# A hybrid encoder block on one core: spread norm factors read in PSUM, and the second FFN's first three weight pieces loaded and split in common tiles during the recurrence

## The chip, the cores and the metric

One core of a Trainium2 chip runs the whole block. The metric is the device time of one execution in microseconds (us); the kernel before takes 1086.48 us, the median of three runs (1085.79 to 1087.56).

## The reference

One residual layer on 512 tokens of width 1024, all in float32: a half-step SwiGLU FFN, a token mixer of two head groups (a gated delta rule and a latent attention), and a second half-step SwiGLU FFN. Each of the three starts with an RMS norm of x that is scaled and shifted per column.

```
h = _rms(x) * (1.0 + s1) + sh1
x = x + 0.5 * g1 * ((silu(h @ gate) * (h @ up)) @ ffn1_w_out)
h = _rms(x) * (1.0 + s2) + sh2
x = x + g2 * (concat(gated_delta_rule(h), latent_attention(h)) @ w_out)
h = _rms(x) * (1.0 + s3) + sh3
x = x + 0.5 * g3 * ((silu(h @ gate) * (h @ up)) @ ffn2_w_out)
```

The FFN is 2816 wide. The delta rule carries a state over the sequence and is worked out in blocks of 128 tokens.

## The kernel before, in words

The activations lie transposed, 128 features on the partitions and 512 tokens along the free axis: x is eight tiles `xT[0..7]`. A product in float32 is done as three matmuls of rounded halves (`mm3`, lines 258 to 261): each operand is split in a high part (a cast on ScalarE, called ACT in the profile) and a low part (operand minus high part on VectorE, DVE). Weights come in **pieces** of 1024 rows by 128 columns: one DMA fills a raw tile `wr`, then line 191 (ACT) casts it to `wh` and line 192 (DVE) subtracts to `wl`. These three tags have four buffers each, in a pool of their own, used in turn. All other 128 by 512 tiles come out of one common pool of 56 ("slots"), used in turn too. PSUM has three accumulators (`psa`) and five auxiliary tiles (`psb`).

The list of pieces is written down in `plan_units`; `prefetch(n)` emits load and split of the next ones until n are ready, and `next_unit` hands one out.

The **norm** before the mixer and before the second FFN is done in two halves of 256 tokens, so that it overlaps the matmuls around it (`norm_half`, line 472). A half goes: column sums of the squares by matmul (line 506), 1/rms on GpSimd (line 177), a diagonal matrix of it (`dg`, line 426, DVE), a matmul of ones by `dg` that spreads the factors over all partitions (line 434, into PSUM), a copy of the result to the slot tile `rb` (line 436, ACT). Then `modulate` does for each of the eight `kt`: x times scale times `rb` (`hm`, line 452, DVE), the shifted sum rounded (`hh`, line 454, ACT), and the low part (`hl`, line 446, DVE).

The work **around the change** runs in this order:

- The recurrence (`recur`, in `mixer`), four steps of 128 tokens; each step's result goes through `gated_out` into the split tiles `mixed` (lines 1373 to 1376). Matmuls of the output projection fill in between.
- `out_half(0)` and `out_half(1)`: for each of eight column groups t, twelve matmuls of 256 tokens, then DVE adds the accumulator to `xT[t]` (line 1723), which frees the accumulator, ACT squares the sum (line 468), and GpSimd or DVE adds it up (`na`, line 470). The four double pieces of `w_out` are held for both halves, so all four `wh`/`wl` buffers are taken until the second half gives them back, one every two t. `out_half(1)` also steps the first half of the norm at t = 1, 2 and 5, and prefetches the second FFN's first three pieces at t = 2, 4 and 6.
- `first_units` (in `ffn2`, and likewise in `latents` for the mixer): three pieces into the three accumulators, first for the 256 tokens of the first half, `kt` by `kt`, then for the second half. The second half of the norm is stepped inside it after 6, 12 and 16 groups of three matmuls. After the first half it prefetches one more piece.

The order of matmuls in these stretches is the program's (`matmuls_in_order`). On the other engines a planner sets the order when the program is built: an engine is given what is ready by the planner's own costs, the earlier in the program first. Each engine then runs its list strictly in that order. The DMAs are issued by SyncE (SP) in one such list.

Of the kernel before, what the change touches and what calls it, by code (L numbers as in the profile page):

```python
# [18 lines left out]
P = 128  # L19
NT = 512  # L20
D = 1024
KT = D // P
NB = NT // P
DFF = 2816
FT = DFF // P
EPS = 1e-6
HALF = NT // 2
KPARTS = ((0, 8), (8, 8), (16, 6))
# [11 lines left out]
class Side:  # L40


    def __init__(self, wide=1):
        self.todo, self.open, self.wide, self.at = [], [], wide, 0
# [21 lines left out]
class Rates:  # L66
# [5 lines left out]
    def step(self, n=1):  # L72
        self.at += n
        for side, r in zip(self.sides, self.rates):
            side.step(int(self.at * r + .01) - int((self.at - n) * r + .01))


class Block:
# [126 lines left out]
    def unit_wide(self, src):  # L205
# [4 lines left out]
        half = lambda w, e: w.rearrange("p (k e) f -> p k e f", k=4)[:, :, e, :]  # L210
        return [(half(hi, e), half(lo, e)) for e in range(2)]

    def unit_krab(self):

        w = self.ins["w_in"][0]
        raw, hi, lo = self.w_tiles()
        self.nc.gpsimd.memset(raw[:, :, 72:], 0.0)
        self.load(raw[:, :, 0:64], w[:, 2696:2760].rearrange("(k p) f -> p k f", p=P))
        self.load(raw[:, :, 64:72], w[:, 2048:2056].rearrange("(k p) f -> p k f", p=P))
        self.split_w(raw, hi, lo)  # L220
        return hi, lo

    def plan_units(self):

        ins = self.ins
        cols = lambda w, c: self.specs.append(lambda: self.unit(w[:, c:c + P]))

        def ffn(w1, w2, first, ts):
            for f in range(first, FT):
                cols(w1, f * P)  # L230
                cols(w1, DFF + f * P)
            for t in ts:
                for k0, n in KPARTS:
                    self.specs.append(lambda k0=k0, n=n, t=t: self.unit(w2[k0 * P:(k0 + n) * P, t * P:(t + 1) * P], n))

        ffn(ins["ffn1_w_in"][0], ins["ffn1_w_out"][0], 3, [*range(KT), KT - 2])
        w = ins["w_in"][0]
        for c in (2056, 2184, 2312, 2440, 2568):
            cols(w, c)
        self.specs.append(self.unit_krab)  # L240
        for c0 in (512, 0, 1024, 1536):
            for h in range(4):
                cols(w, c0 + h * P)
        for r in (4, 0):
            for t in range(0, KT, 2):
                self.specs.append(lambda r=r, t=t: self.unit_wide(ins["w_out"][0][r * P:(r + 4) * P, t * P:(t + 2) * P]))
        ffn(ins["ffn2_w_in"][0], ins["ffn2_w_out"][0], 0, range(KT))

    def prefetch(self, n):
        while len(self.ready) < n and self.specs:  # L250
# [38 lines left out]
    def phase0(self):  # L289

        nc = self.nc
# [50 lines left out]
        dg = self.diag(r)  # L342
# [17 lines left out]
        for kt in range(KT):  # L360
            (hi, lo), (xh, xl) = w, self.h[kt]
            more = kt + 1 < KT
            if kt + 2 < KT:
                loads.append(self.phase0_load(kt + 2))
            if kt == 0:
                for j in range(6):
                    nc.tensor.matmul(pu[j], hi[:, j, :], xh, start=True, stop=False)
                rb = self.spread_diag(dg, NB)
            for j in range(6):
                if j == 0 and more:  # L370
                    cols = self.phase0_cols(kt + 1, loads[kt + 1][0])
                    if kt > 0:
                        w = weights(kt + 1)
                if j == 2 and more:
                    columns(kt + 1, *cols)
                    self.modulate([kt + 1], slice(0, NT), rb, self.c2, self.c1)
                    if kt == 0:
                        w = weights(kt + 1)
                if kt > 0:
                    self.mm3(pu[j], hi[:, j, :], lo[:, j, :], xh, xl, False, kt == KT - 1)  # L380
                else:
                    nc.tensor.matmul(pu[j], hi[:, j, :], xl, start=False, stop=False)
                    nc.tensor.matmul(pu[j], lo[:, j, :], xh, start=False, stop=False)
# [46 lines left out]
    def spread_diag(self, dg, n):  # L430

        nc = self.nc
        pr = self.aux()
        nc.tensor.matmul(pr[:, :n * P], self.ones, dg[:, :n * P], start=True, stop=True)
        rb = self.slot(s="rb")
        nc.scalar.copy(rb[:, :n * P], pr[:, :n * P])
        return rb

    def modulate(self, kts, ts, rb, scale, shift):

# [38 lines left out]
            self.modulate(range(k, k + 2), ts, rb, self.mod[j + 1], self.mod[j])  # L479
            yield  # L480

    def first_units(self, n, nb, lead, marks):


        units = [self.next_unit(ahead=0) for _ in range(n)]
        ps = [self.acc() for _ in range(n)]
        first = [(kt, i) for kt in range(KT) for i in range(lead)] + [(kt, i) for i in range(lead, n) for kt in range(KT)]
        with self.matmuls_in_order(self.last_mm):
            for half in range(2):
                ts = slice(half * HALF, half * HALF + HALF)  # L490
                for at, (kt, i) in enumerate([(kt, i) for kt in range(KT) for i in range(n)] if half else first):
                    self.dense(ps[i], units[i], self.h, ts, kt, kt + 1)
                    if half == 0 and at in marks:
                        next(nb, None)
                if half == 0:
                    drain(nb)
                    self.prefetch(1)
        return ps

    def colsum(self, sq):  # L500
# [216 lines left out]

    def ffn2(self, nb):
        act = []
        ps = self.first_units(3, nb, 3, (5, 11, 15))  # L720
        act.append(self.glu(ps[0], ps[1]))
        act.append(self.glu(ps[2], self.proj(self.aux())))
        for f in range(2, FT):
            pg = self.proj()
            act.append(self.glu(pg, self.proj(), f >= 17))
        self.down(act, self.mod[8])
# [165 lines left out]
    def latents(self, nb):  # L892

        nc = self.nc
        wq = self.up_weight("mla_w_uq", self.vcol["mla_q_norm_w"], 3, 384)
        wkv = self.up_weight("mla_w_ukv", self.vcol["mla_kv_norm_w"], 2, 512)
        next(wq)
        next(wkv)
        ps = self.first_units(3, nb, 3, (5, 11, 15))

        def gather(ps):
            parts, acc = [], None
            for p in ps:
                parts.append(self.split(p, "lat"))
                sq = self.slot(s="lsq")
                nc.scalar.activation(sq, p, AF.Square)
                if acc is None:
                    acc = sq
                else:
                    nc.vector.tensor_tensor(out=acc, in0=acc, in1=sq, op=ALU.add)  # L910
            return parts, acc

        pk = self.proj(self.aux())
        qp, acc = gather(ps)
        ps = [pk]
        lq = qp, self.rms_cols(self.colsum(acc), NB, 384)
        wq = next(wq)
        ps.append(self.proj())
        kp, acc = gather(ps)
        p = self.proj()  # L920
        lkv = kp, self.rms_cols(self.colsum(acc), NB, 256)
        wkv = next(wkv)
        s = self.slot(s="kab")
        nc.scalar.copy(s[:72, :], p[:72, :])
        return lq, wq, lkv, wkv, s
# [642 lines left out]
    def mixer(self, nb):  # L1568
# [93 lines left out]

        na = self.norm_half(0, accum, 6)
        self.mixed[:4] = [(self.slot(F32R, "mh"), self.slot(F32R, "ml")) for _ in range(4)]
        with self.matmuls_in_order():
            gated = Side(wide=NB)
            for p in range(NB):
                while self.wk[p] is None:
                    loosely(chain, 1)
                for _ in self.recur(p):  # L1670
                    loosely(chain, 2)
                    loosely(rest, 4)
                    if not rest.open and not rest.todo:
                        fill.step(3)
                    gated.step(2)
                gated.add(self.gated_out(p))
                gated.step()
                if p == 1:
                    def half():
                        while len(gated.todo) + len(gated.open) > 2:  # L1680
                            yield
                        yield from self.out_half(0, accum)
                    fill.add(half())
            while rest.open or rest.todo:
                loosely(rest, 1)
            fill.step(4)
            gated.flush()
            fill.flush()
            self.new_h()
            drain(self.out_half(1, accum, na))  # L1690
            drain(na)
# [17 lines left out]
    def out_half(self, half, accum, na=None):  # L1709
# [5 lines left out]
        for t in range(KT):  # L1715
            if half == 0 and t % 2 == 0:
                self.wide.append(self.next_unit(ahead=1 if t < 6 else 0))
            if half == 1 and t > 0 and t % 2 == 0:
                self.prefetch(t // 2)
            p = self.acc()  # L1720
            self.dense(p, self.wide[t // 2][t % 2], self.mixed, ts, k1=4, last=3)
            yield
# [41 lines left out]
```

## Time and profile before

| | us |
|---|---|
| median of the runs | 1086.48 |
| the profiled execution | 1085.86 |
| its span | 1084.2 |
| TensorE (PE) busy | 1058.0 (98%) |
| VectorE (DVE) busy | 574.5 (53%) |
| ScalarE (ACT) busy | 390.0 (36%) |
| GpSimd (POOL) busy | 45.1 (4%) |

The span runs from the first to the last instruction; the profiled execution took 1.66 us more than its span. Busy times are sums over the whole program. PE's matmuls overlap, so that a matmul shows 0.28 us while the next one starts 0.12 us later. A number in brackets behind a row of the timeline is the time the engine sat idle before it and what ended that.

### The profile page before, as it was taken

How to read it: one execution, taken by the hardware profiler on the slowest of the kernel's cores; microseconds unless marked ns; L12 is line 12 of the kernel's file. 1: busy time of each engine (PE TensorE's matmuls, PEld its weight loads, DVE VectorE, ACT ScalarE, POOL GpSimd, SP SyncE). 2: the span in 40 equal slices, each digit the busy share in tenths (PEclk: the TensorE clock that was granted, in tenths of full speed). 3: DMA queues.
4: the chain of work that ended last, by engine and by line, in shares of the span. 5: the costliest groups of instructions: out<-in, count | busy, mean ns of one | idle time of the engine just before them, and what ended most of it. 6: DMA issues, size and time to landing. Idle time of an engine off the chain costs nothing.

```text
span 1084.2 us, 14161 instructions
## 1 busy us (share of the span) xinstructions
PE 1058.0 (98%) x5591; PEld 878.1 (81%) x5591; DVE 574.5 (53%) x1021; ACT 390.0 (36%) x643; POOL 45.1 (4%) x96
## 2 busy tenths in 40 slices
PE   6999999999999999998999999999999999999998
PEld 4788878788887899887777778988888888888887
DVE  4488884333587455469868646774333333322220
ACT  4342222222222345475565454444222222222220
POOL 1000000000000010102000031200000000000000
PEclk9999999999999999999999999999999999999999
DMA  9989963332697345211232001124333333333320
GB/s 276 271 253 304 300 192 97 98 97 88 214 289 233 110 122 167 72 39 42 76 72 50 28 14 39 47 71 128 95 97 96 96 97 96 91 104 108 98 73 30
DMA packets 210576, 132.04 MB, mean 122 GB/s; under 512 B 13633, under 2 KB 194638, under 8 KB 210510
## 3 DMA queue, kind: packets, MB, share of 16 engines
q1 hardware_dynamic: 210510, 131.14, 41.3%
q8 instruction: 44, 0.72, 0.3%
q14 instruction: 22, 0.18, 0.1%
HBM read 128.63 MB, written 2.49 MB: 121 GB/s over the span
## 4 chain that ended last, share of the span: by engine, by line
PE 89%; DVE 5%; issue 2%; ACT 1%; DMA 1%; SPq 1%; POOL 0%; POOLq 0%; ACTq 0%
PE pa L259 26%; PE pa L260 25%; PE pa L261 25%; PE pb L1521 1%; PE pb L407 1%; PE pb L259 1%; PE pb L260 1%; PE pb L261 1%; DMA ar<-in_w_ada 1%; PE pb L1144 1%; PE pb L1520 1%; DVE wl L192 1%; PE pb L1537 1%; SPq L116 0%; PE pb L1229 0%
## 5 line engine op out<-in xcount | busy, mean ns | idle before, releaser
L191 ACT CAST wh<-wr 128x1024 fp32r<-128x1024 f32 (+1 forms) x170 | 173.3, 1021 | 501.3 <-PE pa L260 339.7
L259 PE MATMUL pa<-hh,wh 128*128 128x512 f32 (+1 forms) x885 | 339.3, 383 | 4.0 <-DVE xT L1723 2.7
L260 PE MATMUL pa<-hl,wh 128*128 128x512 f32 (+1 forms) x885 | 336.3, 380 | 0.0
L261 PE MATMUL pa<-hh,wl 128*128 128x512 f32 (+1 forms) x885 | 335.9, 380 | 0.0
L192 DVE TENSOR_TENSOR wl<-wr,wh 128x1024 fp32r<-128x1024 f32 (+1 forms) x170 | 201.6, 1187 | 236.5 <-ACT wh L191 230.7
L259 PEld LDWEIGHTS pa<-hh,wh 128*128 128x128 f32 x885 | 167.1, 189 | 39.0 <-issue 3.5
L261 PEld LDWEIGHTS pa<-hh,wl 128*128 128x128 f32 x885 | 167.1, 189 | 31.5 <-issue 0.6
L260 PEld LDWEIGHTS pa<-hl,wh 128*128 128x128 f32 x885 | 167.2, 189 | 29.9 <-issue 0.3
L259 PE MATMUL pa<-ah,wh 128*128 128x512 f32 (+1 forms) x418 | 150.2, 359 | 0.0
L261 PE MATMUL pa<-ah,wl 128*128 128x512 f32 (+1 forms) x418 | 148.8, 356 | 0.0
L260 PE MATMUL pa<-al,wh 128*128 128x512 f32 (+1 forms) x418 | 148.7, 356 | 0.0
L259 PEld LDWEIGHTS pa<-ah,wh 128*128 128x128 f32 x418 | 79.0, 189 | 12.6 <-ACT wh L191 1.7
L261 PEld LDWEIGHTS pa<-ah,wl 128*128 128x128 f32 x418 | 79.0, 189 | 11.4
L260 PEld LDWEIGHTS pa<-al,wh 128*128 128x128 f32 x418 | 79.1, 189 | 11.0
L590 DVE TENSOR_TENSOR af<-sg,pa 128x512 f32<-128x512 f32 x40 | 27.5, 686 | 105.4 <-PE pa L261 104.7
L544 DVE SCALAR_TENSOR_TENSOR aa<-ar,sc,aa 128x512 f32<-128x512 f32 x98 | 73.2, 750 | 13.6 <-DMA ar<-in_w_ada 12.0
L652 DVE SCALAR_TENSOR_TENSOR xT<-pa,mod,xT 128x512 f32<-128x512 f32 (+1 forms) x19 | 12.7, 667 | 48.2 <-PE pa L261 48.1
L259 PE MATMUL pa<-mh,wh 128*128 128x256 f32 (+1 forms) x96 | 31.6, 332 | 0.8 <-ACT mh L1564 0.8
L592 ACT CAST ah<-af 128x512 fp32r<-128x512 f32 x44 | 27.4, 622 | 10.8 <-DVE af L590 10.8
L260 PE MATMUL pa<-ml,wh 128*128 128x256 f32 (+1 forms) x96 | 31.0, 323 | 0.0
L261 PE MATMUL pa<-mh,wl 128*128 128x256 f32 (+1 forms) x96 | 30.8, 320 | 0.0
L593 DVE TENSOR_TENSOR al<-af,ah 128x512 fp32r<-128x512 f32 x44 | 30.2, 686 | 0.7 <-ACT ah L592 0.7
(351 smaller groups left out, 995.5 us busy)
## 6 DMA issues: line engine op xcount, KB each, us to landing
wr<-in_ffn_w_in SPq DMA_DIRECT2D x82, 512.0 KB, 4.0
ar<-in_w_ada SPq DMA_DIRECT2D x48, 512.0 KB, 5.9
wr<-in_ffn_w_out SPq DMA_DIRECT2D x34, 512.0 KB, 4.3
ar<-in_w_ada SPq DMA_DIRECT2D x48, 256.0 KB, 5.3
wr<-in_w_in SPq DMA_DIRECT2D x21, 512.0 KB, 3.8
wr<-in_ffn_w_out SPq DMA_DIRECT2D x17, 384.0 KB, 4.7
wr<-in_w_out SPq DMA_DIRECT2D x8, 512.0 KB, 4.0
wr<-in_ffn_w_in SPq DMA_DIRECT2D x8, 384.0 KB, 7.1
```

The lines of the kernel that those rows point to most:

```text
L191: self.nc.scalar.copy(hi, raw)
L192: self.nc.vector.tensor_tensor(out=lo, in0=raw, in1=hi.bitcast(F32), op=ALU.subtract)
L259: mm(out, wh, xh, start=start, stop=False)
L260: mm(out, wh, xl, start=False, stop=False)
L261: mm(out, wl, xh, start=False, stop=stop)
L407: nc.tensor.matmul(pg[32 * q:32 * q + 32, :256], self.sc[:, kc:kc + 1].to_broadcast([P, 32]), a[:, kc], start=(e == 0), stop=(e == 1), til ...
L544: nc.vector.scalar_tensor_tensor(out=acc, in0=a, scalar=sc, in1=acc, op0=ALU.mult, op1=ALU.add)
L590: nc.vector.tensor_tensor(out=a, in0=s, in1=pu, op=ALU.mult)
L592: nc.scalar.copy(ah, a)
L593: nc.vector.tensor_tensor(out=al, in0=a, in1=ah.bitcast(F32), op=ALU.subtract)
L652: nc.vector.scalar_tensor_tensor(out=self.xT[t][:, ts], in0=p[:, ts], scalar=gate[:, t:t + 1], in1=self.xT[t][:, ts], op0=ALU.mult, op1=AL ...
L1144: nc.tensor.matmul(pa[:, ps], kh[:, ps], x[:, ps], start=True, stop=True)
```

## The change

`spread_diag` returns the PSUM tile instead of a copy of it; `modulate` reads the factors there. Only `phase0`, which uses the factors for longer, still copies them to a slot.

The second FFN's first three pieces leave the list. They are loaded in the loop over the recurrence's steps, one behind each of the first three steps, by the new `unit_halves`: each piece as two slot tiles of four `kt`, each split with the common `split` (a cast on ACT and a subtraction on DVE of 128 by 512). `Halves` makes the two tiles look like one. `out_half(1)` prefetches nothing any more, and `first_units` of the second FFN prefetches three pieces (the list's next) instead of one after its first half. For `latents` nothing changes but the form of the call.

```
+class Halves:
+    def __init__(self, tiles):
+        self.tiles = tiles
+    def __getitem__(self, at):
+        return self.tiles[at[1] // 4][:, at[1] % 4 * P:at[1] % 4 * P + P]
...
+    def unit_halves(self, src):
+        hi, lo = [], []
+        for j in range(2):
+            raw = self.slot(s="fr")
+            self.load(raw.rearrange("p (k f) -> p k f", k=4), src[j * NT:(j + 1) * NT].rearrange("(k p) f -> p k f", p=P))
+            h, l = self.split(raw, "f")
+            hi.append(h)
+            lo.append(l)
+        return Halves(hi), Halves(lo)
...
         ffn(ins["ffn2_w_in"][0], ins["ffn2_w_out"][0], 0, range(KT))
+        first = len(self.specs) - 2 * FT - len(KPARTS) * KT
+        del self.specs[first:first + 3]
...
-                rb = self.spread_diag(dg, NB)
+                rb = self.slot(s="rb")
+                nc.scalar.copy(rb, self.spread_diag(dg, NB))
...
         nc.tensor.matmul(pr[:, :n * P], self.ones, dg[:, :n * P], start=True, stop=True)
-        rb = self.slot(s="rb")
-        nc.scalar.copy(rb[:, :n * P], pr[:, :n * P])
-        return rb
+        return pr
...
-    def first_units(self, n, nb, lead, marks):
-        units = [self.next_unit(ahead=0) for _ in range(n)]
+    def first_units(self, units, nb, lead, marks, ahead):
+        n = len(units)
...
                 if half == 0:
                     drain(nb)
-                    self.prefetch(1)
+                    self.prefetch(ahead)
...
-        ps = self.first_units(3, nb, 3, (5, 11, 15))
+        ps = self.first_units(self.firsts, nb, 3, (5, 11, 15), 3)
...
+        w1 = self.ins["ffn2_w_in"][0]
+        self.firsts = []
...
                 gated.add(self.gated_out(p))
                 gated.step()
+                if p < 3:
+                    self.firsts.append(self.unit_halves(w1[:, (0, DFF, P)[p]:(0, DFF, P)[p] + P]))
...
-            if half == 1 and t > 0 and t % 2 == 0:
-                self.prefetch(t // 2)
```

More of the change, by code (lines that the diff above doesn't have):

```diff
@@ L898, in latents @@
         next(wkv)
-        ps = self.first_units(3, nb, 3, (5, 11, 15))
+        ps = self.first_units([self.next_unit(ahead=0) for _ in range(3)], nb, 3, (5, 11, 15), 1)
         def gather(ps):
```

## The prediction

> **What bounds the kernel now.** I read the page first, then who PE waited for, then the stretches with those waits.
>
> ```profile
> span 1084.2 us, 14161 instructions
> PE 1058.0 (98%) x5591; PEld 878.1 (81%) x5591; DVE 574.5 (53%) x1021; ACT 390.0 (36%) x643; POOL 45.1 (4%) x96
> PE 89%; DVE 5%; issue 2%; ACT 1%; DMA 1%; SPq 1%; POOL 0%; POOLq 0%; ACTq 0%
> ```
>
> PE is the bound. An edit that leaves its matmuls alone can only win where PE waits or runs slowly. The list of PE's waits over the whole execution has four that lie near the change:
>
> ```profile
> PE pa L259 <- DVE xT L1723: 2.7, 2, 2.4
> PE pa L259 <- ACT hh L454: 1.3, 1, 1.3
> PE pb L1321 <- DVE S L1341: 1.1, 1, 1.1
> PE pb L506 <- DVE na L470: 1.0, 1, 1.0
> ```
>
> The first is the entry to the second FFN, the second and fourth the entry to the mixer, the third the recurrence. The busy times of these stretches (PE, weight loads, DVE, ACT, GpSimd, then the granted clock, the DMA share and GB/s):
>
> ```profile
> 400.00:410.00 10.00, 7.72 (x63) 7.34 (x62) 7.59 (x18) 4.27 (x7) 0.88 (x2) 1.00 0.70 174
> 640.00:690.00 50.00, 48.80 (x373) 43.91 (x374) 34.57 (x70) 21.61 (x48) 13.64 (x14) 1.00 0.15 43
> 713.15:718.80 5.65, 5.65 (x34) 5.61 (x34) 5.53 (x14) 2.39 (x5) 0.87 (x1) 0.70 0.30 89
> ```
>
> The last row matters: behind the 2.4 us wait PE is "busy" all the time, but at 0.70 of its clock. The mixer's entry, with waits of 1.3 and 1.0 us, kept 1.00.
>
> **What the second entry loses.** PE's timeline there:
>
> ```profile
> 709.13 0.28 PE L261 MATMUL pa<-mh,wl 128*128 128x256 f32 x1
> 709.25 0.28 PE L259 MATMUL pa<-hh,wh 128*128 128x256 f32 x1
> 710.17 0.39 PE L259 MATMUL pa<-hh,wh 128*128 128x256 f32 x1 [0.29 <-DVE xT L1723]
> 713.15 0.39 PE L259 MATMUL pa<-hh,wh 128*128 128x256 f32 x1 [2.36 <-DVE xT L1723]
> 718.95 0.67 PE L434 MATMUL pb<-dg,ones 128*128 128x256 f32 x2
> ```
>
> From 709.25 to 718.95 PE does the first 12 of `first_units`' groups (36 matmuls) and the second column sum. At the pace of 709.13 to 709.25, 0.12 us, the matmuls take 4.3 us; I give the column sum 0.4. So 4.7 us of work took 9.7: **5.0 us lost**, of which 0.29 + 2.36 = 2.65 idle, 5.65 x 0.30 = 1.7 slow clock, and the rest restarts.
>
> Why: group 2 and 3 write accumulators that `xT` of t = 6 and t = 7 (line 1723) give back, and DVE is late with them. DVE, then ACT:
>
> ```profile
> 701.39 1.22 DVE L192 TENSOR_TENSOR wl<-wr,wh 128x1024 fp32r<-128x1024 f32 x1
> 704.66 1.23 DVE L192 TENSOR_TENSOR wl<-wr,wh 128x1024 fp32r<-128x1024 f32 x1 [0.47 <-ACT wh L191]
> 706.13 0.48 DVE L452 SCALAR_TENSOR_TENSOR hm<-xT,mod,rb 128x256 f32<-128x256 f32 x1
> 707.71 1.22 DVE L192 TENSOR_TENSOR wl<-wr,wh 128x1024 fp32r<-128x1024 f32 x1
> 712.61 0.49 DVE L1723 SCALAR_TENSOR_TENSOR xT<-pa,mod,xT 128x256 f32<-128x256 f32 x1
> 714.46 1.24 DVE L192 TENSOR_TENSOR wl<-wr,wh 128x1024 fp32r<-128x1024 f32 x1
> ```
> ```profile
> 703.58 1.05 ACT L191 CAST wh<-wr 128x1024 fp32r<-128x1024 f32 x1 [2.71 <-PE pa L260]
> 704.85 0.35 ACT L436 COPY rb<-pb 128x256 f32<-128x256 f32 x1
> 709.38 1.05 ACT L191 CAST wh<-wr 128x1024 fp32r<-128x1024 f32 x1
> 731.81 1.05 ACT L191 CAST wh<-wr 128x1024 fp32r<-128x1024 f32 x1 [5.52 <-PE pa L260]
> ```
>
> Three subtractions of 1.22 stand ahead of the last `xT`, which ends at 713.1 though its last matmul started at 709.13. And ACT stood 2.71 us before a cast whose buffer the projection still held, with the copy `rb` queued behind it; the first `hm` waited for that.
>
> **The change, part by part.**
>
> *Factors in PSUM.* Removed: the copy `rb`, four times outside `phase0`. Added: 32 reads of `hm` from PSUM. The trace shows no `hm` with such a read; nearest are these two groups of the same form, from SBUF and with an accumulator in PSUM:
>
> ```profile
> L1723 DVE SCALAR_TENSOR_TENSOR xT<-pa,mod,xT 128x256 f32<-128x256 f32 x16 | 7.6, 483 | 5.4 <-PE pa L261 5.4
> L452 DVE SCALAR_TENSOR_TENSOR hm<-xT,mod,rb 128x256 f32<-128x256 f32 x16 | 7.6, 485 | 1.3 <-ACT rb L436 1.3
> ```
>
> 483 against 485 ns: I take 0, bounds -2 and +2 ns each, nothing over 32. The Trainium skill (VectorE: DVE Perf Modes, "Rules for kernel authors") speaks against the edit: copy PSUM to SBUF first where many operations read it; its table of cycles has 62 more for a PSUM source, by which, as an estimate from that page, eight reads would cost 0.5 us a half; with the two first halves, whose `hm` PE waits for, the sum below would end 1.0 us higher. The rows show no such difference.
>
> The spread tile is held until the last `hm` instead of until the copy. Five auxiliary tiles are used in turn, and between two spreads only a column sum and then the next FFN's or latent's tile are taken, so nobody waits; without that cover the next spread would wait for all eight `hm`, 8 x 0.48 = 3.9 us.
>
> *The three pieces.* They leave the `wr`/`wh`/`wl` buffers. But these buffers do not stay empty: the prefetch of three after the first half gives pieces 3 to 5 the very buffers that pieces 0 to 2 had, free at the same moments. The trace shows what a planner does with a piece of that place in the program: piece 3 was cast at 709.38, at once, long before the norm's rest; but its subtraction came at 714.46, five us after, because DVE had the norm's work, earlier in the program, all the time. So I expect the **casts to return and the subtractions to fall behind** the `xT` and `hm`. The first, at 701.39, has nothing better ready beside it (the spread comes later) and stays.
>
> The sum for the second entry: the last `xT` ends at 713.1 now. Two subtractions go behind it: -2.4; the wait for a cast in front of one: -0.47. That gives 710.2. It cannot end before 709.13 + 0.28 + 0.49 = 709.9. PE wants that accumulator at 709.25 + 6 x 0.12 = 709.97, so it waits 0.2 us. One more subtraction ahead makes 1.4 us, about the mixer entry's 1.3 that left the clock at 1.00. I leave 1.3 us lost in all (the 0.2, some 0.3 of restart, 0.8 for ACT, which still stands before casts with `hh` behind them): gain **3.7**, bounds 0.5 (all three stay) and 5.0.
>
> By the Trainium skill (TensorE: Matmul & The Clock Gate, "What's actually happening") the clock halves only after an idle window of about 3.4 us. Here 0.70 followed waits of 0.29 and 2.36. By the page no stall left over would slow PE; by the row one near 2.4 us does.
>
> What is late next: the second half. Its spread would come some 4 us earlier, and its `hm`/`hl` are wanted only after 24 groups; the two deferred subtractions, 2.4 us, fit there. Pieces 3 to 5 are needed only after `first_units` ends, where now the cast at 731.81 takes the first buffer given back; nothing is exposed.
>
> *The mixer's entry*, where only the copy goes:
>
> ```profile
> 391.76 0.60 PE L434 MATMUL pb<-dg,ones 128*128 128x256 f32 x2
> 392.75 0.96 DVE L192 TENSOR_TENSOR wl<-wr,wh 128x768 fp32r<-128x768 f32 x1 [1.16 <-ACT wh L191]
> 393.63 0.88 DVE L452 SCALAR_TENSOR_TENSOR hm<-xT,mod,rb 128x256 f32<-128x256 f32 x2
> 404.44 0.36 PE L259 MATMUL pa<-hh,wh 128*128 128x256 f32 x1 [1.30 <-ACT hh L454]
> ```
>
> The factors are in PSUM at 392.36. The first `hm` can come up to 1.27 us earlier, but DVE is idle only from then to 392.75, and is nearly full until PE's stall. Gain **0.4**, bounds 0 and 1.3.
>
> *The recurrence* takes on six loads of 256 KB, six casts, six subtractions. The nearest rows for these operations:
>
> ```profile
> L592 ACT CAST ah<-af 128x512 fp32r<-128x512 f32 x44 | 27.4, 622 | 10.8 <-DVE af L590 10.8
> L593 DVE TENSOR_TENSOR al<-af,ah 128x512 fp32r<-128x512 f32 x44 | 30.2, 686 | 0.7 <-ACT ah L592 0.7
> SPq L116 <- DVE wl L192: 127.0, 18, 27.6
> L544 DVE SCALAR_TENSOR_TENSOR aa<-ar,sc,aa x39: 744/752/754, 279.8 to 348.0; 128x512 f32<-128x512 f32 x39
>   DMA ar<-in_w_ada: 10.2, 8
> 255.00:350.00 95.00, 95.00 (x425) 77.73 (x424) 61.46 (x82) 23.30 (x28) 2.43 (x9) 1.00 0.70 225
> ```
>
> ACT gets 6 x 0.62 = 3.7 us, DVE 6 x 0.69 = 4.1. From 640 to 690 DVE idles 50 - 34.57 = 15.4 and ACT 28.4, so there is room, but each engine runs in order and the state update stands behind whatever is put ahead: PE already waited 1.1 us for `S`. If each of six subtractions is in the way by half its length, DVE is 2.1 us late, of which PE, filled with the projection's matmuls, sees perhaps a third: loss **0.6** (a choice). Below nothing it cannot go, as no work leaves this stretch. Above: a cast or subtraction set in the list where its load hasn't landed. That happened to the slot loads of the first FFN: DVE waited 10.2 us in 8 times, 1.3 each; six times is 7.7 us. SP's list is in order too, and SP stood 127.0 us in 18 times (from 640 to 800) for a `wr` to come free; a slot load queued behind such a wait comes late.
>
> **The sum.** -3.7 - 0.4 + 0.6 = -3.5. The profiled execution took 1085.86 (its span 1084.2 and 1.7 around it), so 1082.4; the median of the runs lies 0.6 above that execution, which gives **1083.0 us**.
>
> **Rivals.**
>
> *The splits return whole* (the change doesn't do what it says): pieces 3 to 5 are subtracted where pieces 0 to 2 were, since DVE is free for a moment at each cast's end. For it: the buffers come free at the same times, and casts are taken at once. Against: piece 3's five us of delay. The second entry then gains only 0.5, and -0.5 - 0.4 + 0.6 gives 1086.2. Chance 0.22.
>
> *Everything goes*: the casts, too, fall behind, PE meets no stall (5.0), the mixer's entry gains 0.9, the recurrence loses 0.3: -5.6, 1080.9. For it: DVE idles 15.4 us in the recurrence. Against: the first subtraction's place at 701.39. Chance 0.14.
>
> *The recurrence pays*: the slot splits stand before their loads, `S` behind them. If all 7.7 us come through to PE, -3.7 - 0.4 + 7.7 = +3.6, 1090.1. It makes the kernel slower by over 0.2% once more than 4.1 + 2.2 = 6.3 of the 7.7 us come through. For it: 1.3 us for each such wait before; against: the DMAs carried 225 GB/s in that stretch, against 43 here. Chance 0.14.
>
> **How the numbers follow.** My forecast holds 0.50, with 1081.5 to 1085 as its own range. A measurement of this kernel can tell about 0.2%, 2.2 us: faster means below 1084.3, slower above 1088.7. Faster: 0.40 of the forecast's 0.50 and 0.14. Slower: 0.12 of the last rival's 0.14. Same: the rest, 0.34. The range goes from 1080.6 (everything goes, and a little) to 1087.6 (the splits return and the recurrence costs two of its waits); outside lies most of the last rival and a little below.
>
> **What would show it.** Right: no wait of PE for `xT` over 1 us at the entry to the second FFN, the granted clock 1.00 behind it, the last `xT` near 710, `hm` right behind the spread matmul at equal length, at most one 128x1024 subtraction before that `xT`. The first rival: three of them there. The recurrence: DVE or ACT waiting for a DMA into `fr`, PE's wait for `S` above 1.1. I am wrong if the second entry keeps its idle time, or if `hm` grows.

## The result and the profile after

The changed kernel takes 1096.4 us (median of 4 runs, 1093.87 to 1097.28), the kernel before 1086.1 (4 runs, 1085.03 to 1087.56): the ratio on record is **1.0077** (95% interval 1.0051 to 1.0103); the two medians by themselves give 1.0095. It is slower. Forecast were 1083.0 us, range 1080.6 to 1087.6; the result lies above the range.

The profiled execution of the changed kernel took 1097.28 us. Its page, and the list of PE's waits over the whole execution (total, times, longest, in us). Functions that the diff doesn't touch stand 22 to 24 lines lower in the changed kernel: L259 is now L282, L1367 is L1389, L1723 is L1747, L882 is L904.

```profile
span 1095.6 us, 14167 instructions
PE 1062.9 (97%) x5591; PEld 881.8 (80%) x5591; DVE 573.8 (52%) x1024; ACT 389.8 (36%) x642; POOL 46.1 (4%) x96
...
PE pb L1389 <- DVE on L904: 8.0, 3, 4.0
...
PE pb L528 <- DVE na L492: 1.5, 2, 1.0
PE pb L458 <- DVE dg L450: 1.2, 1, 1.2
PE pa L282 <- ACT hh L476: 1.1, 1, 1.1
PE pa L282 <- DVE xT L1747: 0.9, 2, 0.5
```

PE stays the bound, and the wait at its head is new: three times in the recurrence, 8.0 us in all, PE stands before the transposes of `on` (line 1389), which DVE has not yet made. The wait for `S`, 1.1 us before, is gone from the list. The entry to the second FFN waits less for `xT` (0.9 against 2.7) and newly for `dg` (1.2) and `na` (0.5 of the 1.5). The mixer's entry waits 1.1 us for `hh` instead of 1.3.

To split the 11.4 us between the two profiled executions by place, three matmuls that both have in the same order of PE's list: the first on `S` behind the first step, the transposes of the last step, the second half's spread of the norm factors. PE's timeline before, then after (start, length):

```profile
660.18 1.05 PE L1321 MATMUL pb<-S,w 128*128 128x128 f32 x8
690.32 0.63 PE L1367 MATMUL pb<-ident,on 128*128 128x128 f32 x4
```
```profile
664.61 1.05 PE L1343 MATMUL pb<-S,w 128*128 128x128 f32 x8
703.23 0.63 PE L1389 MATMUL pb<-ident,on 128*128 128x128 f32 x4
730.50 0.67 PE L458 MATMUL pb<-dg,ones 128*128 128x256 f32 x2 [1.19 <-DVE dg L450]
```

With 718.95 for the spread before, the changed kernel is 4.4 us late at the first mark, 12.9 at the second, 11.6 at the third and 11.4 at the end. So the recurrence costs **8.5 us**, the second FFN's entry gains **1.4**, and 4.4 us are lost ahead of the first piece's casts and subtractions. These 4.4 are the clock. The stretch from 640 to 650 (PE, weight loads, DVE, ACT, GpSimd, granted clock, DMA share, GB/s), before and after:

```profile
640.00:650.00 10.00, 9.85 (x101) 8.65 (x102) 6.25 (x11) 4.00 (x7) 6.89 (x7) 1.00 0.01 2
```
```profile
640.00:650.00 10.00, 10.00 (x67) 8.34 (x66) 3.89 (x8) 1.39 (x4) 5.26 (x6) 0.50 0.00 0
650.00:655.00 5.00, 5.00 (x34) 4.71 (x34) 2.54 (x3) 2.74 (x4) 0.00 (x0) 0.77 0.11 28
```

10 x 0.50 + 5 x 0.23 is some 6.1 us of clock lost; the changed kernel was 1.6 us ahead at the wait just before (638.53 against 640.15), which leaves 4.5, near the 4.4. Of the recurrence's 8.5 us, 8.0 - 1.1 = 6.9 are more idle time of PE, and 1.7 are slow clock behind the longest of the waits (0.80 and 0.86 from 680 to 690). Whether that clock comes with the change is a question for the runs below.

**What the recurrence waits for.** ACT and DVE in its first changed step, after:

```profile
667.06 1.06 ACT L201 CAST wh<-wr 128x1024 fp32r<-128x1024 f32 x1 [2.55 <-PE pa L283]
```
```profile
664.83 0.69 DVE L900 TENSOR_TENSOR fl<-fr,fh 128x512 fp32r<-128x512 f32 x1
667.29 0.75 DVE L1731 SCALAR_TENSOR_TENSOR xT<-pa,mod,xT 128x512 f32<-128x512 f32 x1 [1.77 <-PE pa L284]
668.15 1.23 DVE L202 TENSOR_TENSOR wl<-wr,wh 128x1024 fp32r<-128x1024 f32 x1
669.29 0.68 DVE L900 TENSOR_TENSOR fl<-fr,fh 128x512 fp32r<-128x512 f32 x1
669.89 0.68 DVE L1345 TENSOR_TENSOR vn<-uu,pb 128x512 f32<-128x512 f32 x1
670.49 0.69 DVE L904 TENSOR_TENSOR on<-o,ry 128x512 f32<-128x512 f32 x1
```

and DVE in the same step before:

```profile
661.27 0.69 DVE L1323 TENSOR_TENSOR vn<-uu,pb 128x512 f32<-128x512 f32 x1 [0.80 <-PE pb L1321]
661.87 1.24 DVE L882 TENSOR_TENSOR on<-o,ry 128x512 f32<-128x512 f32 x1
663.03 0.73 DVE L1705 SCALAR_TENSOR_TENSOR xT<-pa,mod,xT 128x512 f32<-128x512 f32 x1
664.27 1.23 DVE L192 TENSOR_TENSOR wl<-wr,wh 128x1024 fp32r<-128x1024 f32 x1 [0.50 <-ACT wh L191]
```

The new subtractions are `fl`, 0.69 us each. What matters is not their length but that the order of the older work has turned over. Before, `vn` and `on` came first, and then `xT` and `wl` of a `w_out` piece, which wait for PE and for ACT's cast. After, `fl`, `xT`, `wl` and the second `fl` all stand ahead of `vn` and `on`: DVE idles 1.77 us before an `xT` for which PE isn't ready, and the `wl` behind it could start no sooner than ACT's `wh` ended, at 668.12, which itself stood 2.55 us for PE to give back its buffer. The matmuls on `S` end at 664.61 + 1.05 = 665.7; `vn` follows four us later. In the next step ACT stands 3.73 us and PE waits the 4.0 us of the list. No queue is late: each `fr` was loaded before its cast was due, and none of the six casts and six subtractions has an idle time in front of it.

### The profile page after: what moved, and what is told of

It reads as the page before. It is cut to its first block, busy times and chain, and to the rows that moved or that the text cites. A ratio compares the mean times of both kernels' runs of the same rounds, so it can differ in the third digit from the quotient of the medians.

```text
span 1095.6 us, 14167 instructions
## 1 busy us (share of the span) xinstructions
PE 1062.9 (97%) x5591; PEld 881.8 (80%) x5591; DVE 573.8 (52%) x1024; ACT 389.8 (36%) x642; POOL 46.1 (4%) x96
## 4 chain that ended last, share of the span: by engine, by line
PE 88%; DVE 5%; issue 2%; ACT 2%; DMA 1%; SPq 0%; POOL 0%; ACTq 0%; POOLq 0%
PE pa L282 25%; PE pa L283 25%; PE pa L284 25%; PE pb L1543 1%; DMA ar<-in_w_ada 1%; PE pb L282 1%; PE pb L283 1%; PE pb L284 1%; PE pb L431 1%; PE pb L1166 1%; PE pb L1542 1%; DVE wl L202 1%; PE pb L1559 1%; ACT wh L201 0%; SPq L126 0%
## 5 line engine op out<-in xcount | busy, mean ns | idle before, releaser
L201 ACT CAST wh<-wr 128x1024 fp32r<-128x1024 f32 (+1 forms) x167 | 170.6, 1023 | 503.7 <-PE pa L283 348.6
L282 PE MATMUL pa<-hh,wh 128*128 128x512 f32 (+1 forms) x837 | 324.5, 388 | 1.1 <-ACT hh L476 1.1
L283 PE MATMUL pa<-hl,wh 128*128 128x512 f32 (+1 forms) x837 | 322.0, 385 | 0.0
L284 PE MATMUL pa<-hh,wl 128*128 128x512 f32 (+1 forms) x837 | 321.7, 384 | 0.0
L202 DVE TENSOR_TENSOR wl<-wr,wh 128x1024 fp32r<-128x1024 f32 (+1 forms) x167 | 197.8, 1186 | 228.7 <-ACT wh L201 222.8
L282 PEld LDWEIGHTS pa<-hh,wh 128*128 128x128 f32 x837 | 157.3, 188 | 35.5 <-issue 3.5
L284 PEld LDWEIGHTS pa<-hh,wl 128*128 128x128 f32 x837 | 157.3, 188 | 31.4 <-issue 0.6
L283 PEld LDWEIGHTS pa<-hl,wh 128*128 128x128 f32 x837 | 157.5, 188 | 30.2 <-issue 0.3
L282 PE MATMUL pa<-ah,wh 128*128 128x512 f32 (+1 forms) x418 | 150.1, 359 | 0.0
L282 PEld LDWEIGHTS pa<-ah,wh 128*128 128x128 f32 x418 | 79.0, 189 | 12.6 <-ACT wh L201 1.7
L284 PEld LDWEIGHTS pa<-ah,wl 128*128 128x128 f32 x418 | 79.0, 189 | 11.4
L282 PE MATMUL pa<-mh,wh 128*128 128x256 f32 (+1 forms) x96 | 32.1, 337 | 0.8 <-ACT mh L1586 0.8
```

What stands on the lines that cost most here:

```text
L201: self.nc.scalar.copy(hi, raw)
L202: self.nc.vector.tensor_tensor(out=lo, in0=raw, in1=hi.bitcast(F32), op=ALU.subtract)
L282: mm(out, wh, xh, start=start, stop=False)
L283: mm(out, wh, xl, start=False, stop=False)
L284: mm(out, wl, xh, start=False, stop=stop)
```

## The experiments

Every kernel below ran in several rounds beside the kernel before on the same chip; each ratio is to that, as on record; it can differ by 0.001 or so from the quotient of the medians. The mean granted clock is the mean over the runs of a kernel. It differs between runs of one kernel (0.989 to 1.000 for the kernel before), and the time moves with it, so one column gives the median of time x granted clock, a rough estimate of what the run would have taken at full clock. The last two columns come from PE's timeline of the profiled execution: the recurrence, from the first matmul on `S` behind the first step to the transposes of the last, and the entry to the second FFN, from the first half's spread of the norm factors to the second half's. The first profile of the changed kernel has 38.62 and 16.05 there.

| kernel | ratio (95%) | median us | mean clock | time x clock | recurrence | entry |
|---|---|---|---|---|---|---|
| before, beside e1 to e4, e5 to e8, e9 to e12 | 1 | 1087.9, 1087.9, 1086.3 | 0.9944, 0.9944, 0.9953 | 1081.8, 1081.8, 1082.4 | 30.14 | 17.42 |
| changed, again (e5) | 1.0055 (1.0035 to 1.0075) | 1094.7 | 0.9945 | 1089.1 | 40.28 | 16.06 |
| factors alone (e1) | 0.9977 (0.9957 to 0.9998) | 1085.5 | 0.9970 | 1083.6 | 30.16 | 17.31 |
| factors alone, again (e9) | 0.9984 (0.9966 to 1.0001) | 1085.5 | 0.9974 | 1083.2 | 30.15 | 17.30 |
| pieces alone (e2) | 1.0091 (1.0064 to 1.0118) | 1098.5 | 0.9915 | 1089.4 | 40.59 | 17.47 |
| splits behind `vn`, `on` (e3) | 1.0009 (0.9989 to 1.0029) | 1088.6 | 0.9972 | 1086.2 | 34.01 | 15.90 |
| splits ahead of the loop (e4) | 1.0020 (1.0003 to 1.0036) | 1090.1 | 0.9945 | 1084.3 | 30.15 | 16.05 |
| one piece (e6) | 1.0002 (0.9986 to 1.0018) | 1089.4 | 0.9947 | 1083.5 | 31.89 | 15.90 |
| loads only in the loop (e7) | 1.0043 (1.0025 to 1.0062) | 1094.0 | 0.9913 | 1083.9 | 30.15 | 19.18 |
| splits behind `S` and `o` (e8) | 1.0001 (0.9984 to 1.0019) | 1088.4 | 0.9974 | 1085.6 | 33.84 | 15.90 |
| one piece, early (e10) | 0.9983 (0.9965 to 1.0000) | 1084.6 | 0.9971 | 1081.9 | 30.25 | 15.90 |
| the same, `dg` first (e11) | 0.9962 (0.9945 to 0.9979) | 1082.7 | 0.9972 | 1080.0 | 30.28 | 15.10 |
| factors, `dg` first (e12) | 0.9982 (0.9964 to 1.0001) | 1084.4 | 0.9970 | 1082.2 | 30.14 | 17.01 |

**The two parts apart (e1, e2).** The kernel before with only the spread factors left in PSUM:

```diff
...
-        rb = self.slot(s="rb")
-        nc.scalar.copy(rb[:, :n * P], pr[:, :n * P])
-        return rb
+        return pr
```

> The spread factors read in PSUM, the pieces left as before. Theory (the loss sits in the recurrence, where the subtractions of the slot pieces put vn and on late on DVE): no loss here, PE has no wait for `on` at line 1367's counterpart in the recurrence over 1.7 us, and the copies' absence gives 0 to 1.5 us: 1085.5 (1084.5 to 1087). Rival (reading the factors in PSUM makes hm slower): hm above 0.55 us against 0.485, 1088 or more.

and the changed kernel with these lines put back:

> The three pieces loaded and split in the recurrence, the copy of the spread factors kept. Theory: the whole loss, PE waits for `on` of 2.5 to 4 us twice and over 1 us once in the recurrence, 1094 to 1098. Rival (the factors in PSUM carry the loss): 1083 to 1087. Rival (the slow clock from 640 to 652 is chance and makes most of the loss): this run's profile may lack it, and then it ends at 1090 to 1092.

The factors alone are 0.9977, the pieces alone 1.0091. The whole loss belongs to the pieces (1098.5 us, just above the expected 1094 to 1098), and the rival that PSUM slows `hm` is out. The groups of `hm` and PE's waits from 600 to 765 with the factors alone:

```profile
L451 DVE SCALAR_TENSOR_TENSOR hm<-xT,mod,pb 128x256 f32<-128x256 f32 x32 | 14.9, 476 | 2.9 <-PE pb L435 2.9
...
PE pa L259 <- DVE xT L1722: 2.5, 3, 1.7
...
PE pb L435 <- DVE dg L427: 1.4, 1, 1.4
PE pb L1320 <- DVE S L1340: 1.0, 1, 1.0
```

476 ns where the SBUF source had 483: the read from PSUM costs nothing. The recurrence has its old wait for `S` and none for `on`. The second FFN's entry is not less idle, it idles 3.9 us instead of 2.65; but in three shorter waits for `xT`, the longest 1.7 instead of 2.4. From spread to spread the entry takes 17.31 us against 17.42, and the recurrence is unchanged. What the two measurements of this kernel support is a gain of 1.7 to 2.5 us by their ratios (0.8 and 2.4 by the medians), with intervals that end at about no change. Time x clock is 1.8 us above the kernel before on the same chip, and the mean clock is 0.0026 higher, 2.8 us of 1085, which would put the gain on the clock; no profile shows where it lies.

With the pieces alone, PE's waits in the same stretch are those of the changed kernel in the recurrence and those of the kernel before at the entry:

```profile
PE pb L1390 <- DVE on L905: 8.0, 3, 4.0
PE pa L282 <- DVE xT L1748: 2.6, 2, 2.4
```

So the entry's 2.4 us for `xT` goes only with both parts together: with the pieces alone three subtractions of 1.22 us still stand ahead of the last `xT` (714.43, 717.70 and 720.75), and with the factors alone three as well.

The kernel with the pieces alone also shows what the slow clock at the entry was worth. The stretch from the entry's first matmul to the second spread, in the kernel before, with the pieces alone, and in the changed kernel:

```profile
709.25:718.95 9.70, 7.05 (x43) 6.44 (x41) 9.43 (x25) 4.85 (x10) 0.87 (x1) 0.82 0.37 109
```
```profile
722.30:732.04 9.74, 5.55 (x42) 4.91 (x41) 9.45 (x25) 4.83 (x10) 0.87 (x1) 1.00 0.37 107
```
```profile
722.17:730.50 8.33, 5.71 (x43) 4.92 (x41) 8.30 (x22) 4.54 (x9) 0.69 (x1) 1.00 0.23 66
```

With the pieces alone PE has the two waits for `xT` of before, but the clock stays at 1.00; the stretch still takes 9.74 us, because PE then waits 1.55 us for `dg` instead. DVE is busy for nearly the whole of each of the three: it bounds the entry, and the slow clock of before cost next to nothing there.

**Order or work (e3, e8).** The changed kernel, with the same loads, casts and subtractions in the same loop. Only, the splits of a piece are written one step later and put behind `vn` and `on` on DVE and behind `o` on ACT, as an order without any wait:

```diff
-                    self.firsts.append(self.unit_halves(w1[:, (0, DFF, P)[p]:(0, DFF, P)[p] + P]))
+                    raws.append(self.raw_halves(w1[:, (0, DFF, P)[p]:(0, DFF, P)[p] + P]))
...
+                    if k == 0 and p:
+                        with self.traced() as late:
+                            self.firsts.append(self.split_halves(raws.pop(0)))
+                        for i in late:
+                            if i.engine == dve:
+                                self.follow(i, on(own, dve)[-1])
+                                self.follow(i, on(out, dve)[0])
+                            if i.engine == act:
+                                self.follow(i, on(own, act)[-1])
```

(`raw_halves` loads, `split_halves` casts and subtracts; `own` holds the step's `vn` and `o`, `out` the `on` of the step before.)

> The changed kernel with the same loads, casts and subtractions in the same loop, but each piece's split written behind vn and on of the next step (an order on DVE, and behind o on ACT, without any wait). Theory (it is the place in the lists of DVE and ACT that costs, not the work): the 8.5 us that the recurrence lost go, PE's waits for `on` there fall to 1 us or less, 1084 to 1088. Rival (the work itself, 3.7 us of ACT and 4.1 us of DVE, or its loads, are what the recurrence cannot take): 1092 or more. Rival (the slow clock before the recurrence is the loss): the clock 0.5 from 640 to 650 stays and it ends at 1089 to 1092.

In e8 the splits come another half step later, behind the state update and the step's output (the orders are then behind the last DVE operation of that part, and on ACT behind `o`; the line as e3 has it, and as e8 has it):

```diff
-                    if k == 0 and p:
+                    if k == 1 and p:
```

> As the third experiment, but each split is written behind the state update S and the output of its step as well. Theory: PE's wait for S falls from 2.6 to about 1.1 us, waits for `on` stay at 1 us or less, and the time ends 1 to 2 us below the third experiment's, 1086 to 1088. Rival (what is left in the third experiment is not these waits): no difference to its 1088.6.

PE's waits from 600 to 765 in e3, then in e8:

```profile
PE pb L1357 <- DVE S L1377: 2.6, 2, 2.3
PE pb L1403 <- DVE on L918: 1.9, 2, 1.2
```
```profile
PE pb L1403 <- DVE on L918: 3.3, 3, 1.5
...
PE pb L1357 <- DVE S L1377: 1.0, 1, 1.0
```

and DVE in e3, ahead of its longest wait for `S`:

```profile
667.78 1.29 DVE L914 TENSOR_TENSOR fl<-fr,fh 128x512 fp32r<-128x512 f32 x2
668.98 0.68 DVE L1377 TENSOR_TENSOR S<-Sg,pb 128x512 f32<-128x512 f32 x1
```

The ratio falls from the changed kernel's 1.0055 and 1.0077, taken beside other runs, to 1.0009, a difference of 5 to 7 us with some 3 us of uncertainty. PE's timeline says it more closely: the recurrence takes 34.01 us instead of 38.62 and 40.28, so **4.6 to 6.3 us of its loss are the order** (with the slow clock behind the long waits), with not one operation less on PE, DVE or ACT. The theory's condition on `on` (1 us or less) was missed by 0.2, and its 1084 to 1088 us by 0.6. What remains is 3.9 us in e3 and 3.7 in e8. It is put down to the work: DVE is full at these places (4.90 to 4.96 of 5 us from 665 to 670, 675 to 680 and 684 to 689 in e3), and the same subtractions now delay `S` (e3) or `on` (e8), 4.5 and 4.3 us of waits against 1.1. Moving the place again gained nothing (1088.4 against 1088.6), as e8's rival had it.

**The dose (e6).** Only the first piece in common tiles, the other two as before.

```diff
-        del self.specs[first:first + 3]
+        del self.specs[first:first + 1]
...
-                if p < 3:
+                if p < 1:
...
```

> Only the first of the three pieces is loaded and split in the recurrence, the other two as before. Theory (each piece's split in front of vn and on costs its own step): PE waits 2.5 to 3 us for `on` in the first of these steps and not in the later ones, 1087 to 1091. Rival (any such split upsets the recurrence as a whole, or the loss is elsewhere): two or three waits for `on`, 1094 or more.

PE's waits from 600 to 765:

```profile
PE pb L1389 <- DVE on L904: 2.7, 1, 2.7
...
PE pb L458 <- DVE dg L450: 1.2, 1, 1.2
...
PE pa L282 <- DVE xT L1749: 0.7, 2, 0.5
PE pb L528 <- DVE na L492: 0.5, 1, 0.5
```

One wait of 2.7 us, in the step that has the piece: each piece costs its own step, this one 1.75 us of the recurrence's time. And the entry is as good as with all three pieces, 1.2 + 0.7 + 0.5 = 2.4 us of waits: the second and the third piece bought nothing there.

**Loads or splits (e7), and the splits ahead (e4).** In e7 the loads stay in the loop, and the twelve casts and subtractions come behind it:

```diff
-                    self.firsts.append(self.unit_halves(w1[:, (0, DFF, P)[p]:(0, DFF, P)[p] + P]))
+                    self.firsts.append(self.raw_halves(w1[:, (0, DFF, P)[p]:(0, DFF, P)[p] + P]))
...
             gated.flush()
             fill.flush()
+            self.firsts = [self.split_halves(f) for f in self.firsts]
```

> The three pieces are loaded in the recurrence as in the changed kernel, but cast and subtracted only behind the loop. Theory: PE's waits for `on` in the recurrence are gone, the twelve casts and subtractions lie at the second FFN's entry where DVE has some 5 us free ahead of the norm: 1085 to 1089. Rival (the loads, or the common tiles they hold, are the loss): the waits in the recurrence stay, 1093 or more.

In e4 all three pieces are loaded and split ahead of the loop:

```diff
-        self.firsts = []
+        self.firsts = [self.unit_halves(w1[:, c:c + P]) for c in (0, DFF, P)]
...
-                if p < 3:
-                    self.firsts.append(self.unit_halves(w1[:, (0, DFF, P)[p]:(0, DFF, P)[p] + P]))
```

> The changed kernel with all three pieces loaded and split ahead of the loop over the recurrence's steps, and nothing of them in it. Theory: the order in the recurrence is that of the kernel before, the second FFN's entry that of the changed kernel (2.6 us idle instead of 5.0 lost): 1082 to 1085. Rival (the splits only move the loss to the work ahead of the first step): waits of PE for uu, w or S between 645 and 665, 1088 or more.

PE's waits in e7, then in e4, and ACT's timeline in e4:

```profile
PE pb L472 <- DVE dg L464: 3.6, 1, 3.6
PE pb L542 <- DVE na L506: 2.1, 1, 2.1
```
```profile
PE pb L1366 <- ACT uu L1322: 2.6, 1, 2.6
```
```profile
652.85 0.62 ACT L899 CAST fh<-fr 128x512 fp32r<-128x512 f32 x1 [2.81 <-DMA fr<-in_ffn_w_in]
...
657.88 1.07 ACT L1322 COPY uu<-pb 128x512 f32<-128x512 f32 x2
```

In e7 the loads and the tiles they hold do no harm: no wait for `on` is left in the recurrence, which takes 30.15 us as before. That answers the rival, though the time does not, at 1.0043: the splits then meet the norm of the second FFN on DVE, and PE waits 3.6 us for `dg` and 2.1 for `na`. The expected 5 us of free DVE there were a misreading, and the 1085 to 1089 us were missed. In e4 the mechanism that the prediction had feared for the recurrence does appear, in another place: ACT stands before loads that haven't landed, with `uu` queued behind them. Its rival was right.

**The clock ahead of the loop (e5).** The changed kernel as it is:

> The changed kernel itself, once more. Theory (the order in the recurrence makes the loss; the clock of 0.50 from 640 to 652 in its first profile is no effect of the change): PE's three waits for `on` of 8.0 us in all are there again, the clock from 640 to 650 is 1.00, and the time still lies 1092 to 1098. Rival (the slow clock there comes with the change): 0.50 from 640 to 650 again.

Its windows, and PE's three marks:

```profile
640.00:650.00 10.00, 9.95 (x102) 8.75 (x103) 6.25 (x10) 4.07 (x8) 6.79 (x7) 1.00 0.01 2
665.00:670.00 5.00, 3.24 (x16) 3.27 (x17) 3.35 (x10) 1.23 (x5) 0.00 (x0) 0.66 0.78 211
680.00:685.00 5.00, 4.42 (x24) 4.29 (x24) 3.65 (x11) 1.11 (x4) 0.00 (x0) 0.66 0.76 207
```
```profile
660.05 1.05 PE L1343 MATMUL pb<-S,w 128*128 128x128 f32 x8
...
700.33 0.63 PE L1389 MATMUL pb<-ident,on 128*128 128x128 f32 x4
...
727.59 0.67 PE L458 MATMUL pb<-dg,ones 128*128 128x256 f32 x2 [1.20 <-DVE dg L450]
```

The clock is 1.00 from 640 to 650: the slow stretch of the first profile does not belong to the change. The loss is there without it, and so it is in the profile of the pieces alone, which also has 1.00 there and took 1098.83 us. By the marks the recurrence now costs 10.0 + 0.1 = 10.1 us, of which 7.9 - 1.1 = 6.8 are more idle time of PE and 2 x 5 x 0.34 = 3.4 slow clock behind these waits; the entry gains 1.4 as before.

**A version that beats both (e9 to e12).** In the trace of the kernel before, DVE idles 1.49 us between the first step's `S` and `gs`, and ACT 2.61 us behind its `o` and `hn`; one piece fits there. e10 loads the third piece ahead of the loop and splits it in that gap (`raws` is loaded before the loop, the other two pieces stay as they were); e11 also puts the subtractions of the pieces fetched ahead behind the second half's `dg`; e12 has that last order on the factors alone; e9 is e1 again, to stand on the same chip.

```diff
+                for k, _ in enumerate(self.recur(p)):
+                    if p == 0 and k == 1:
+                        self.firsts.append(self.split_halves(raws))
...
+                    with self.traced() as block:
+                        self.prefetch(ahead)
+                    for i in block:
+                        if i.engine == mybir.EngineType.DVE:
+                            self.follow(i, self.dg)
```

> The first experiment's kernel once more (factors in PSUM alone), to stand beside the next three on one chip: ratio to the kernel before 0.996 to 0.999 if its gain is real, 1.000 to 1.001 if it was chance.

> Factors in PSUM, and one piece (the third) in common tiles, loaded ahead of the loop and split right behind the first step, where DVE and ACT idle. Theory: no wait for `on` over 1.2 us and for S over 1.3 in the recurrence, PE's waits at the second FFN's entry are those of the one-piece kernel (1.2 + 0.7 + 0.5 = 2.4 against 3.9 us in the first experiment): 1 to 1.5 us below the kernel with the factors alone, ratio about 0.996. Rival (even this split in a gap of DVE and ACT delays vn): a wait for `on` of 1 to 3 us, no better than the factors alone.

> The same with the subtraction of the piece fetched ahead set behind the second half's dg on DVE. Theory: PE's wait for dg falls from 1.2 to under 0.5 us, some 0.7 us below the kernel without it. Rival (dg waits for the sums and the root ahead of it, not for that subtraction): the wait stays at 1.2 us and so does the time.

> The factors alone, with that same order of the subtraction behind dg. Theory: PE's wait for dg falls from 1.4 to under 0.5 us, some 0.9 us below the kernel with the factors alone. Rival: the wait stays, no difference.

PE's waits of 600 to 765 in e11, the two that matter here, and DVE in the gap:

```profile
PE pb L1361 <- DVE S L1381: 1.1, 1, 1.1
...
PE pb L472 <- DVE dg L464: 0.4, 1, 0.4
```
```profile
658.73 1.30 DVE L918 TENSOR_TENSOR fl<-fr,fh 128x512 fp32r<-128x512 f32 x2 [1.34 <-ACT fh L917]
```

e11 is the only kernel here whose whole interval lies more than 0.2% below the kernel before: 0.9962 (0.9945 to 0.9979), 1082.7 us against 1086.3 on that chip; the changed kernel loses 6 to 8 us to the kernel before by its ratios. The recurrence of e11 has no wait for `on` any more, `S` costs what it did before, and `dg` falls from 1.2 to 0.4. e10 without the line for `dg` lies 0.9 us below the factors alone by the medians, less than the interval can tell, and by the ratios nothing. That e11 lies 2.0 us below e10, where 0.7 was expected, is only in part explained: its entry is 0.8 us shorter. It was measured in one group of runs, and as the best of several. e12, where `dg` still waits 1.1 us, as its rival had it, gains nothing that can be told from e9.

## Why the prediction was wrong

**The recurrence** is the step that failed. Its term was a loss of 0.6 us; the two profiles show 8.5 and 10.1. "Each of six subtractions is in the way by half its length" prices the added work alone and takes the order of the rest as fixed. The list was written anew around the six subtractions, and `vn` and `on` went behind `xT`, `wl` and a cast that wait for PE. Of the loss, e3 gives 4.6 to 6.3 us to that order; the work itself, put behind, still costs 3.9 us (e3) or 3.7 (e8), so that 0.6 would have been too low even with the order kept. The 15.4 us that DVE idled between 640 and 690 were real, but they lay where DVE waits for PE and not where the pieces come.

The **upper bound** of that term, 7.7 us, was too low as well, and built on something that did not happen: loads not landed. The rival "the recurrence pays" was right in its sign and its place, and its 7.7 us for the recurrence were near; its 1090.1 us for the whole was 6.3 too low, and its mechanism was wrong: it had `S` behind the splits, and PE waited for `on`. Its chance of 0.14 leaned on the DMA's load, which e7 shows had no part.

**The second entry** was forecast to gain 3.7 and gained 1.4. Point by point: the casts returned, and of the three subtractions ahead of the last `xT` two stayed (714.30 and 720.20) where at most one was forecast and the first rival had all three; the last `xT` came early, though less than said (it ended at 724.14; less the 12.9 us by which the kernel was then late that is 711.2, where 710.2 was forecast and 713.1 had been); PE waited 0.9 us for `xT` in two waits of at most 0.5, and the clock stayed at 1.00. What failed is that the two deferred subtractions "fit there", behind it. From its first matmul to the second spread the stretch takes 730.50 - 722.17 = 8.3 us against 9.7, so of the 5.0 us lost before 3.6 are still lost, not 1.3. DVE was full from 720 to 735, and the second half's `na` (0.5) and `dg` (1.2) came late instead: PE's idle time in the stretch is 2.6 us, as before, and the prediction had named that as a sign of being wrong. e11, with the subtractions behind `dg`, brought 0.8 of it back. The working ahead of it had misread the stretch, too. It counted 1.7 us of slow clock as lost beside PE's waits; with the pieces alone the clock was 1.00 and the stretch as long, since DVE, busy 9.4 of 9.7 us, was what bounded it.

**The mixer's entry**, 0.4 forecast: the wait for `hh` fell from 1.3 to 1.1, 0.2 us; a size, well within 0 to 1.3. `hm` from PSUM at no cost held: 478 ns in the changed kernel against 483. The Trainium skill's advice to copy PSUM to SBUF first where many operations read it (VectorE: DVE Perf Modes, "Rules for kernel authors") had been weighed at 1.0 us and put aside; the trace does not show that cost.

Together: e5's profiled execution, whose clock was undisturbed ahead of the loop, took 1094.38, 8.5 us more than the one before, where -3.5 was forecast. The 12.0 us between are 10.1 - 0.6 = 9.5 in the recurrence, 3.7 - 1.4 = 2.3 at the entry and 0.2 at the mixer.

What the prediction could have read from the trace of the kernel before: DVE's wait of 0.80 ahead of `vn` (line 1323) and PE's of 1.1 for `S` say that in the first steps the chain PE, `vn`, PE, `S` has nothing to spare. Work set into such a chain must be priced by what it can push ahead of the chain's next link, not by its length; here that was an `xT`, which waited 1.6 to 2.4 us for PE, and a `wl` whose cast had waited 2.6 and 3.7.

## What to carry to other kernels

Before work is moved to a stretch because an engine idles there, look at what each idle time of that engine waits for: idle time in a serial chain is no room, except in gaps where the next link is not yet due, as behind the first step's `S`, where e10 put its piece. Where a planner writes the lists, an added operation can turn the order of the old ones, so pin the chain's links ahead of the new work and read the order again. Move only as much as the place it leaves needs: one piece of three brought all that the entry gained. And where PE waits, look first whether another engine is full in that stretch: at the entry only less work ahead of `dg` on DVE made it shorter.

## What the hardware showed that was not expected

**The granted clock falls by chance after short waits.** In the first profile of the changed kernel it fell to 0.50 for 10 us and more after two waits of 0.78 and 1.60 us, 3.7 us apart; e6, e7 and e8 had it at the same place, the kernel before and the other nine profiles had the same two waits and kept 1.00. By the windows from 635 to 655 such a stretch costs 5 to 7 us. Longer waits do the same: behind one of 2.4 us the clock was 0.70 in the kernel before and 1.00 with the pieces alone, behind one of 2.7 us 0.66 in e5 and 1.00 in the first profile. Behind the 4.0 us all three profiles that have this wait show a slow clock, 0.66 to 0.80 in the slowest 5 us. The Trainium skill (TensorE: Matmul & The Clock Gate, "What's actually happening") says that the clock falls after an idle window of about 3.4 us and that the window runs free of the kernel. The free window would account for the chance; the length does not agree, as no single wait ahead of the loop reached 1.7 us.

So the time of one kernel moves with its mean clock, which lay between 0.989 and 1.000 over the runs of the kernel before. But a slow stretch does not always cost what its clock says: the one at the entry to the second FFN cost next to nothing, because DVE set the pace there. Whether the factors in PSUM gain by the clock (its mean is 0.002 to 0.003 higher with them) is not shown: no profile of theirs has a part that is shorter by as much.
